# A hybrid attention and RWKV-7 layer on one core: 2 KB buffers of 2080 bytes, smaller constants, and the scores of a head pair issued ahead of the low parts of k

## The chip, the cores and the metric

The kernel runs on one core of a Trainium2 chip. The metric is the device time of one execution in microseconds (us). The kernel before took 1186.74 us, the median of 3 runs that lie between 1185.92 and 1186.84 us.

## The reference, cut to what matters

One decoder layer on 512 tokens of width 2048. The normed input goes through one input projection; its columns feed an attention with three dilations and an RWKV-7 recurrence; each branch has a gate; one output projection follows, then the residual and a final norm.

```python
h = rms_norm(x, norm_g[l])
proj = jnp.matmul(h, w_in[l]).astype(jnp.float32)
q, k, v, z_att, u_shift, z_rwkv = jnp.split(proj, splits, axis=-1)
att = dilated_mixture_attention(q, k, v, pos) * jax.nn.silu(z_att)
rwk = rwkv7_time_mix(u_shift, z_rwkv, ...)
mix = jnp.concatenate([att, rwk], axis=-1).astype(x.dtype)
x = x + jnp.matmul(mix, w_out[l])
return rms_norm(x, final_g)
```

Of the attention: 16 heads of 64 are taken as 8 pairs; q and k are rotated, the scores of a pair are masked, put through exp and divided by their sum, and the result is multiplied with v. Of the RWKV part only this matters here: `k = k * (1.0 + (a - 1.0) * k_a)`, with one constant `k_a` for each of 1024 channels.

## The kernel before, in words

Every float32 operand of a large matmul is split into a high part and a low part, and each product is three matmuls: `hh,whi`, `hl,whi` and `hh,wlo`, where `hh` and `hl` are the two parts of the normed input and `whi`, `wlo` those of a weight. The weights stream in by DMA as `raw` tiles; ScalarE (ACT) copies out `whi`, VectorE (DVE) subtracts to get `wlo`. The columns of the projection come in the order lora, k, r, v of the RWKV part, its gate z0 to z7 beside the recurrence, then q and k of the attention (`mm_qk`), then its gate (`mm_z`, z8 to z15), and then the output projection (`mo`, `mt`, `mh`).

Nothing on the chip picks the order of the work. The program is written out by a planner that runs while it is built. It keeps a model of every engine and queue (`Model`, `Engine`, `Tensor`, `Queue`, lines 42 to 134): each call to an engine moves that engine's modelled end and notes when its result will be ready. The main stream issues the large matmuls one after the other; after each, the side jobs whose time has come by the model are run a step further. A side job is a generator; `yield lat, a, b` means that it goes on when the model's clock has reached the modelled readiness of `a` and `b` plus `lat`. Which of DVE and ACT takes a copy out of PSUM, and which side job comes next, is decided by these modelled times. So a change of a modelled time by a tenth of a microsecond can move instructions anywhere behind it. On the chip each engine runs its own list in the order in which it was issued, and waits by semaphores.

The side jobs that matter here:

- `assemble` (from line 994) builds q or k of a pair: 8 DMAs on the queue of SyncE (SP) move rows of the rotated tiles `m` into `qa` or `ka`; for k, ACT then copies `kd` (high part) and DVE subtracts `kl` (low part).
- `att` (from line 1029) handles two pairs in units of 128 queries: score matmuls `s` (from `q` with `kd`, then with `kl`), a mask and maximum on DVE (`nm`), exp on ACT (`ss`, its sum `den`), a division on DVE, transposes on TensorE (`pt`), copies of these by ACT into `pa` and `pb`, and, two units behind the last one, the product `po` from `pa` and `pb`. The first unit of a pair waits by line 1043.
- `gate_g` loads a piece `gw` of a weight, splits it into `gh`, `gl` and issues four matmuls `pg`. `gate` evacuates a z into `zz` and `zt` and multiplies it with a row of y or with its attention output `yl`, which comes back from DRAM by DMA.

Most intermediates live in two rotating sets of buffers, 20 slots of 2 KB (`k2`) and 9 slots of 4 KB (`k4`). A new tile takes the slot that came free longest ago, and its first writer waits for the last reader of the slot's old content.

Of the kernel before, what the change touches and what calls it, by code (L numbers as in the profile page):

```python
# [11 lines left out]
F32 = mybir.dt.float32  # L12
F32R = mybir.dt.float32r
I32 = mybir.dt.int32
AF = mybir.ActivationFunctionType
ALU = mybir.AluOpType
# [4 lines left out]
P = 128  # L21
# [11 lines left out]
PV = {}  # L33
# [5 lines left out]
NPV = _o  # L39
# [97 lines left out]
def hymba_kernel(ctx: ExitStack, tc: tile.TileContext, xT, x, wa, wb, wo, pv, w2a2, g2, fg,  # L137
                 cst, rope, amask, bmask, out):
    nc = tc.nc
    ctx.enter_context(tc.manual_schedule())  # L140
    model = Model()
    V = Engine(model, nc.vector, 0.07, 0.00106, 0.18)
    S = Engine(model, nc.scalar, 0.06, 0.00095, 0.25)
# [6 lines left out]
    cp = ctx.enter_context(tc.tile_pool(name="cp", bufs=1))  # L150
    wp = ctx.enter_context(tc.tile_pool(name="wp", bufs=3))
    kp = ctx.enter_context(tc.tile_pool(name="kp", bufs=1))
# [5 lines left out]
    K1N, K2N, K4N, RAWN, AHEAD = 5, 20, 9, 2, 2  # L158

    def k2(shape, name, dt=F32):  # L160
        t = kp.tile([P, 528], dt, tag="k2", bufs=K2N, name=name)
        t = t[:, 0:math.prod(shape[1:])]
        return t if len(shape) == 2 else t.rearrange("p (a b) -> p a b", b=shape[2])

    def k1(shape, name, dt=F32):
        return kp.tile(shape, dt, tag="k1", bufs=K1N, name=name)
# [1 line left out]
    def k4(shape, name, dt=F32):  # L168
        return kp.tile(shape, dt, tag="k4", bufs=K4N, name=name)

    def ps(name, shape=(P, 512)):
        return pp.tile(list(shape), F32, tag="ps", name=name)

    def small(shape, name, bufs=12, dt=F32):
        return sp.tile(shape, dt, tag=f"s{shape[1]}", bufs=4 if shape[1] == 4 else bufs, name=name)

    pvt = cp.tile([P, 112], F32, name="pvt")
    nc.scalar.dma_start(pvt[:, 0:NPV], pv)

    def col(n, i):  # L180
        return pvt[:, PV[n] + i:PV[n] + i + 1]
# [5 lines left out]
    gmask = [csts[:, 320:448], csts[:, 448:576]]  # L187
    bmt = cp.tile([P, 2 * P], F32, name="bmt")
    ones = k2([P, P], "ones")
    V.memset(ones, 1.0)  # L190
    bonesr = cp.tile([P, P], F32R, name="bonesr")
    hw0 = cp.tile([P, 32], F32, name="hw0")
    omu = cp.tile([P, 27], F32, name="omu")
    V.tensor_scalar(omu, pvt[:, 0:27], -1.0, 1.0, ALU.mult, ALU.add)
    warm = small([P, 1], "warm")
    S.activation(warm, ones[:, 0:1], AF.Tanh)

    hth, htl, normed = [], [], []
    rstd = cp.tile([P, T], F32, name="rstd")
    rtok = cp.tile([P, 16], F32, name="rtok")[:, 0:4]  # L200
    xt_b, xq_b, Lb = [], [], []

    def prologue():
        acc = k2([P, T], "acc")
        xs = []

# [49 lines left out]
    def later():  # L256
        bones = k2([P, P], "bones")
        Q.dma_start(bones, cst[:, 576:704])
        Q.dma_start(bmt, bmask)
        yield 1.59, bones  # L260
        V.tensor_copy(bonesr, bones)
        V.tensor_scalar(hw0[:, 0:16], pvt[:, PV["w0"]:PV["w0"] + 16], 0.5, None, ALU.mult)
        V.tensor_scalar(hw0[:, 16:24], pvt[:, PV["k_a"]:PV["k_a"] + 8], -1.0, None, ALU.mult)
        for i in range(2):
            G.memset(xt_b[i], 0.0)
            G.tensor_copy(Lb[i][H[i], :, H[i]], ident[H[i], H[i]][:, None, :].to_broadcast([64, NCH, C]))
            yield 0.5, G
# [136 lines left out]
    def start(gen, *wait, rank=1):  # L404
        sides.append([gen, wait_for(*(wait or (0.0,))), rank])
# [161 lines left out]
    def spill_out(key, t):  # L567
        d = dp.tile([P, T], F32, name=f"sp_{key}")
        Q.dma_start(d, t)
        spill[key] = d  # L570
# [57 lines left out]
    def pre(p, r, k, v):  # L628
# [35 lines left out]
        a = k2([P, T], f"a{p}")  # L664
# [44 lines left out]
        V.tensor_scalar(rn2, rn2, 1e-24, None, ALU.max)  # L709
        V.reciprocal(rn2, rn2)  # L710
        start(subst(p, Mp, rn2), 0.06, Mp, rn2, rank=-1)
        S.activation(a, a, AF.Identity, bias=hw0[:, 16 + p:17 + p], scale=col("k_a", p))
        V.scalar_tensor_tensor(k, a, 1.0, k, ALU.add, ALU.mult)
        rk = k2([P, T], f"rk{p}")
        V.scalar_tensor_tensor(rk, r, col("r_k", p), k, ALU.mult, ALU.mult)
# [212 lines left out]
    def att_mask(t):  # L928
        return (am[0][:, 0:128], am[0][:, 128:384], am[1][:, 0:384], am[2])[t]
# [99 lines left out]
    def two(pa, t):  # L1029
        o = 256 if t == 3 else 0  # L1030
        return pa[:, o:o + 768].rearrange("p (j c) -> p j c", j=2)[:, :, t * P - o:t * P - o + P]

    def att(g):
        units = [(2 * g + pr_, t) for pr_ in range(2) for t in range(4)]
        po, ssb_, pts = {}, {}, {}
        for u in range(len(units) + 2):
            if u < len(units):
                pair, t = units[u]
                while pair not in ready or (t == 0 and u == 0 and pair >= 2 and pair - 1 not in scored):
                    yield 0.5  # L1040
                tl_ = pairs[pair]
                if t == 0:
                    yield 0.1, tl_["q"], tl_["kl", 0], tl_["kl", 1]
                n = max(256, 128 * (t + 1))
                nv = 128 * (t + 1)
                tsl = slice(t * P, (t + 1) * P)
                for h in range(2):
                    sc = ps(f"s{pair}{h}{t}")
                    TE.matmul(sc[:, 0:n], tl_["q"][:, h, tsl], tl_["k", h][:, 0:n], start=True, stop=False)
                    TE.matmul(sc[:, 0:n], tl_["q"][:, h, tsl], tl_["kl", h][:, 0:n], start=False, stop=True)  # L1050
                    ss = k2([P, T], f"ss{pair}{h}{t}")
                    nm = small([P, 1], f"nm{pair}{h}{t}")
                    V.tensor_tensor_reduce(ss[:, 0:nv], sc[:, 0:nv], att_mask(t), -0.125, 3.0e38,
                                           ALU.add, ALU.min, accum_out=nm)
                    den = small([P, 1], f"den{pair}{h}{t}")
                    S.activation(ss[:, 0:nv], ss[:, 0:nv], AF.Exp, bias=nm, scale=-1.0, accum_out=den)
                    ssb_[u, h] = (ss, den)
                if t == 3:
                    scored.add(pair)
            if u >= 2:  # L1060
                pair, t = units[u - 2]
                if t == 3:
                    po[pair] = pm.tile([P, T], F32, tag="mm", name=f"po{pair}")
                    for j in range(4):
                        for h in range(2):
                            hd = (2 * pair + h) * 64
                            pa, pb = pts[pair, h]
                            pj = (pa[:, 0:512], pa[:, 512:896], pb[:, 0:256], pb[:, 256:384])[j]
                            TE.matmul(po[pair][H[h], j * P:T], vt[j][:, hd:hd + 64], pj,
                                      start=(j == 0), stop=(j == 3))  # L1070
                if t == 3:
                    if f"s{pair}" in spill:
                        o = yl.pop(pair)
                        V.tensor_tensor(o, o, po.pop(pair), ALU.mult)
                    else:
                        o = k2([P, T], f"o{pair}")
                        S.copy(o, po.pop(pair))
                    spill_out(f"o{pair}", o)
                elif t == 2 and f"s{pair}" in spill:
                    fetch_y(pair, f"s{pair}")  # L1080
            if 1 <= u <= len(units):
                pair, t = units[u - 1]
                for h in range(2):
                    ss, den = ssb_.pop((u - 1, h))
                    if t == 0:
                        pts[pair, h] = (k4([P, 1024], f"pa{pair}{h}"), k2([P, T], f"pb{pair}{h}"))
                    pa, pb = pts[pair, h]
                    pt = ps(f"pt{pair}{h}{t}")
                    for j in range(t + 1):
                        TE.transpose(pt[:, j * P:(j + 1) * P], ss[:, j * P:(j + 1) * P], ident)  # L1090
                    if t == 0:
                        S.copy(pa[:, 0:P], pt[:, 0:P])
                    else:
                        S.copy(two(pa, t),
                               pt[:, 0:2 * P].rearrange("p (j c) -> p j c", j=2))
                    if t >= 2:
                        S.copy(pb[:, (t - 2) * P:(2 * t - 3) * P], pt[:, 2 * P:(t + 1) * P])
            yield 0.0, S
            if u < len(units):
                for h in range(2):  # L1100
                    ss, den = ssb_[u, h]
                    nv = 128 * (units[u][1] + 1)
                    V.reciprocal(den, den)
                    V.tensor_scalar(ss[:, 0:nv], ss[:, 0:nv], den, None, ALU.mult)
            yield 0.0, V
# [13 lines left out]
    def fetch_y(idx, key):  # L1119
        y = k2([P, T], f"yl{idx}")  # L1120
        Q.dma_start(y, spill[key])
        yl[idx] = y
# [53 lines left out]
            yield 1.05  # L1176

    fgt = []
    ssq = cp.tile([P, 4, 8], F32, name="ssq")
    yt = {}  # L1180

    def residual(nb):
# [247 lines left out]
```

## Time and profile before

| what | value |
|---|---|
| median of 3 runs | 1186.74 us |
| the profiled execution | 1185.99 us |
| its span, first to last instruction | 1183.9 us |
| TensorE (PE) busy | 1146.4 us, 97% of the span |
| DVE busy | 735.2 us, 62% |
| ACT busy | 568.6 us, 48% |
| GpSimd (POOL) busy | 336.4 us, 28% |
| mean granted TensorE clock | 0.993 of full |

Rows of a timeline give the start, the duration, the engine, the line in the code, the operation with its output and inputs, and in brackets the idle time ahead of it and what ended it. All engine instructions go through one helper and so share line 88 or 121 (matmuls); tiles are told apart by name. Buffer numbers are left out of the names.

### The profile page before, as it was taken

What the parts mean: (1) busy time and instruction counts of PE and PEld (TensorE: products, weight loads), DVE (VectorE), ACT (ScalarE), POOL (GpSimd) and SP (SyncE); (2) the same over time, 40 slices, a digit from 0 to 9 for tenths busy, and PEclk for the clock granted to TensorE, in tenths of its full rate; (3) what the DMA queues carried; (4) which work ended last, traced back from release to release, by engine and by line L of the source; (5) the groups of instructions that cost most, each with busy time, mean ns of one, the idle gap of its engine ahead of it and who ended that gap; (6) DMA issues with size and microseconds to landing.
All of it is one profiled execution on the core that took longest, in us unless ns stands there. A gap on an engine that the chain in (4) does not pass through costs nothing. (4 is left out here: it accounts for less than half of the span.)

```text
span 1183.9 us, 19123 instructions
## 1 busy us (share of the span) xinstructions
PE 1146.4 (97%) x6878; PEld 938.2 (79%) x6878; DVE 735.2 (62%) x1511; ACT 568.6 (48%) x1254; POOL 336.4 (28%) x586
## 2 busy tenths in 40 slices
PE   7999999999999999999999999999996999999997
PEld 5788777777787777777899977777875778888897
DVE  6667887787767957768743457665655566243252
ACT  6455665645558464564433345544443445232143
POOL 1004885647328470754630001101010000011020
PEclk9999999999999999999999999999998999999999
DMA  7334333242342525234242454433452336444343
GB/s 260 118 92 130 120 105 84 84 126 84 94 136 73 139 65 151 77 100 114 59 121 59 118 166 133 132 109 116 134 142 84 116 113 213 125 125 129 103 125 143
DMA packets 89870, 139.62 MB, mean 118 GB/s; under 512 B 37936, under 2 KB 47664, under 8 KB 89776
## 3 DMA queue, kind: packets, MB, share of 16 engines
q1 hardware_dynamic: 89344, 137.83, 39.1%
q8 instruction: 54, 0.88, 0.3%
q10 hardware_dynamic: 432, 0.58, 0.1%
q14 instruction: 40, 0.33, 0.1%
HBM read 114.44 MB, written 14.75 MB: 109 GB/s over the span
## 5 line engine op out<-in xcount | busy, mean ns | idle before, releaser
L88 POOL TENSOR_TENSOR Xtmp<-XT,Mp 128x248 f32<-128x248 f32 (+30 forms) x248 | 128.9, 520 | 143.6 <-DVE XT L88 112.8
L88 POOL TENSOR_TENSOR XT<-XT,Xtmp 128x248 f32<-128x248 f32 (+30 forms) x248 | 144.6, 583 | 21.4 <-DVE XT L88 2.5
L121 PE MATMUL mm_z<-hh,wlo 128*128 128x512 f32 x256 | 104.1, 407 | 0.0
L121 PE MATMUL mm_z<-hl,whi 128*128 128x512 f32 x256 | 103.2, 403 | 0.0
L121 PE MATMUL mm_qk<-hh,whi 128*128 128x512 f32 x256 | 102.2, 399 | 0.8 <-ACT gtok L88 0.8
L121 PE MATMUL mm_qk<-hl,whi 128*128 128x512 f32 x256 | 102.8, 401 | 0.0
L121 PE MATMUL mm_z<-hh,whi 128*128 128x512 f32 x256 | 102.7, 401 | 0.0
L88 DVE TENSOR_TENSOR wlo<-raw_o,whi 128x512 fp32r<-128x512 f32 x64 | 48.0, 790 | 87.6 <-ACT whi L88 87.6
L121 PE MATMUL mm_qk<-hh,wlo 128*128 128x512 f32 x256 | 102.1, 399 | 0.0
L88 POOL TENSOR_TENSOR y<-y,fg 128x512 f32<-128x512 f32 (+1 forms) x16 | 19.3, 1237 | 272.0 <-ACT mo L88 214.1
L88 ACT ACTIVATE whi<-raw_o 128x512 fp32r<-128x512 f32 x64 | 36.8, 623 | 96.5 <-PE mo L121 73.2
L88 POOL TENSOR_TENSOR m<-m,m 128x512 f32<-128x512 f32 x16 | 22.9, 1451 | 197.7 <-DVE m L88 92.5
L88 ACT ACTIVATE ss<-ss,nm 128x128 f32<-128x128 f32 (+3 forms) x64 | 35.5, 556 | 87.0 <-DVE nm L88 87.0
L121 PE MATMUL mo<-whi,ml 128*128 128x512 f32 x192 | 75.8, 395 | 0.0
L121 PE MATMUL mo<-whi,mh 128*128 128x512 f32 x192 | 75.8, 395 | 0.0
L121 PE MATMUL mo<-wlo,mh 128*128 128x512 f32 x192 | 75.8, 395 | 0.0
L88 DVE TENSOR_TENSOR wlo<-raw_v,whi 128x352 fp32r<-128x352 f32 (+1 forms) x80 | 50.3, 655 | 35.2 <-ACT whi L88 33.9
L88 DVE TENSOR_TENSOR wlo<-raw_z,whi 128x512 fp32r<-128x512 f32 x64 | 48.1, 771 | 33.2 <-ACT whi L88 32.9
L88 DVE TENSOR_TENSOR wlo<-raw_qk,whi 128x512 fp32r<-128x512 f32 x64 | 46.5, 745 | 32.2 <-ACT whi L88 32.1
L121 PE MATMUL mv<-whi,hh 128*128 128x352 f32 x192 | 62.7, 327 | 1.5 <-DVE m L88 1.5
L88 ACT ACTIVATE whi<-raw_v 128x352 fp32r<-128x352 f32 (+1 forms) x80 | 40.8, 542 | 46.5 <-PE mv L121 33.5
L121 PE MATMUL mv<-wlo,hh 128*128 128x352 f32 x192 | 62.2, 324 | 0.0
(303 smaller groups left out, 3043.8 us busy)
## 6 DMA issues: line engine op xcount, KB each, us to landing
raw_z<-in_wa_dram SPq DMA_DIRECT2D x32, 512.0 KB
raw_qk<-in_wa_dram SPq DMA_DIRECT2D x32, 512.0 KB
raw_o<-in_wo_dram SPq DMA_DIRECT2D x32, 512.0 KB
raw_v<-in_wb_dram SPq DMA_DIRECT2D x24, 352.0 KB
raw_r<-in_wa_dram SPq DMA_DIRECT2D x16, 512.0 KB
raw_v<-in_wa_dram SPq DMA_DIRECT2D x16, 512.0 KB
raw_k<-in_wa_dram SPq DMA_DIRECT2D x15, 512.0 KB
xk<-in_xT_dram SPq DMA_DIRECT2D x16, 256.0 KB
```

What stands on the lines that cost most here:

```text
L88: return fn(o, *args, **kw)
L121: return fn(o, lhs, rhs, **kw)
```

## The change

The `k2` slots, 2112 bytes long before (a tile of 528 floats of which a part was used), are tiles of the asked shape; the largest of them has 8 x 65 floats, so the slots become 2080 bytes. Five constants lose unused columns or get tiles of their own: `pvt` 448 to 396 bytes, `rtok` 64 to 16, `ssq` 128 to 80, and `warm` moves from one set of small tiles to the constants. The scaled constants from `w0` and `k_a`, which shared the tile `hw0`, go into two tiles: `hw0` (64 bytes) and a new `nka` of 256 bytes per partition, of which 8 columns are used. In `att` the first unit of a pair waits for `kl` of both heads alone, no longer for `q`, and with a latency of -1.5 in place of 0.1: it may be issued 1.5 us ahead of the time at which the model has `kl` ready.

```diff
     def k2(shape, name, dt=F32):
-        t = kp.tile([P, 528], dt, tag="k2", bufs=K2N, name=name)
-        t = t[:, 0:math.prod(shape[1:])]
-        return t if len(shape) == 2 else t.rearrange("p (a b) -> p a b", b=shape[2])
+        return kp.tile(shape, dt, tag="k2", bufs=K2N, name=name)
...
-    pvt = cp.tile([P, 112], F32, name="pvt")
-    nc.scalar.dma_start(pvt[:, 0:NPV], pv)
+    pvt = cp.tile([P, NPV], F32, name="pvt")
+    nc.scalar.dma_start(pvt, pv)
...
-    hw0 = cp.tile([P, 32], F32, name="hw0")
+    hw0 = cp.tile([P, 16], F32, name="hw0")
+    nka = cp.tile([P, 64], F32, name="nka")
...
-    warm = small([P, 1], "warm")
+    warm = cp.tile([P, 1], F32, name="warm")
...
-    rtok = cp.tile([P, 16], F32, name="rtok")[:, 0:4]
+    rtok = cp.tile([P, 4], F32, name="rtok")
...
-        V.tensor_scalar(hw0[:, 0:16], pvt[:, PV["w0"]:PV["w0"] + 16], 0.5, None, ALU.mult)
-        V.tensor_scalar(hw0[:, 16:24], pvt[:, PV["k_a"]:PV["k_a"] + 8], -1.0, None, ALU.mult)
+        V.tensor_scalar(hw0, pvt[:, PV["w0"]:PV["w0"] + 16], 0.5, None, ALU.mult)
+        V.tensor_scalar(nka[:, 0:8], pvt[:, PV["k_a"]:PV["k_a"] + 8], -1.0, None, ALU.mult)
...
-        S.activation(a, a, AF.Identity, bias=hw0[:, 16 + p:17 + p], scale=col("k_a", p))
+        S.activation(a, a, AF.Identity, bias=nka[:, p:p + 1], scale=col("k_a", p))
...
                 if t == 0:
-                    yield 0.1, tl_["q"], tl_["kl", 0], tl_["kl", 1]
+                    yield -1.5, tl_["kl", 0], tl_["kl", 1]
...
-    ssq = cp.tile([P, 4, 8], F32, name="ssq")
+    ssq = cp.tile([P, 4, 5], F32, name="ssq")
```

The numbers of instructions on PE, POOL and SP stay. What moves is their order, at three places below. Names carry a number of the pair, the head and the unit (`s602`: pair 6, head 0, unit 2), and at their end a running number of the tile.

The first place is the first score of pair 0, where `mm_qk10` ends. On TensorE before:

```order
L121 MATMUL mm_qk10_7255<-hh15_222,wlo101_7225 128x512
L121 MATMUL mm_qk11_7400<-hh0_106,whi102_7291 128x512
L121 MATMUL mm_qk11_7400<-hl0_107,whi102_7291 128x512
L121 MATMUL mm_qk11_7400<-hh0_106,wlo102_7292 128x512
L121 MATMUL mm_qk11_7400<-hh1_118,whi102_7291 128x512
L121 MATMUL s000_7413<-kd_000_7374,q_00_7329 128x256
L121 MATMUL s000_7413<-kl_000_7375,q_00_7329 128x256
```

On TensorE now, the same scores:

```order
L121 MATMUL mm_qk10_7256<-hh14_217,wlo101_7226 128x512
L121 MATMUL s000_7388<-kd_000_7375,q_00_7330 128x256
L121 MATMUL s000_7388<-kl_000_7376,q_00_7330 128x256
L121 MATMUL s010_7396<-kd_001_7379,q_00_7330 128x256
L121 MATMUL s010_7396<-kl_001_7380,q_00_7330 128x256
L121 MATMUL mm_qk10_7256<-hh15_223,whi101_7225 128x512
L121 MATMUL mm_qk10_7256<-hl15_224,whi101_7225 128x512
L121 MATMUL mm_qk10_7256<-hh15_223,wlo101_7226 128x512
```

The scores moved up by seven of the large matmuls. On DVE behind the same scores, before (`g32s` belongs to the gates' weights, `ISA` is the mask and maximum):

```order
L88 TENSOR_TENSOR kl_001_7379<-ka_001_7284,kd_001_7378 128x512
L88 TENSOR_TENSOR m0_10_7403<-mm_qk10_7255,L0_233 128x512
L88 TENSOR_TENSOR m3_10_7405<-mm_qk10_7255,L0_233 128x512
L88 TENSOR_TENSOR g32s_7408<-dup32_7337,g32s_7408 32x512 x2
L88 ISA ss000_7416,nm000_7417<-s000_7413,L1_236 128x128
```

And now:

```order
L88 TENSOR_TENSOR kl_001_7380<-ka_001_7283,kd_001_7379 128x512
L88 ISA ss000_7391,nm000_7392<-s000_7388,L1_237 128x128
L88 ISA nm000_7392 128x1
L88 ISA ss010_7399,nm010_7400<-s010_7396,L1_237 128x128
L88 ISA nm010_7400 128x1
L88 TENSOR_TENSOR g32s_7416<-dup32_7338,g32s_7416 32x512 x2
```

The mask and maximum of unit 0 moved ahead of `g32s`.

The second place is SP's queue where q and k of pair 7 (`qa_31x`, `ka_31x`) are put together. Before, behind the first six of the eight `qa` transfers:

```order
L133 DMA qa_311_9262<-m0_30_8633 32x512
L133 DMA qa_311_9262<-m2_30_8747 32x512
L133 DMA ka_310_9267<-m0_31_8882 32x512
L133 DMA ka_310_9267<-m2_31_9056 32x512
L133 DMA ka_310_9267<-m0_31_8882 32x512
L133 DMA ka_310_9267<-m2_31_9056 32x512
L133 DMA ka_311_9272<-m0_31_8882 32x512
L133 DMA ka_311_9272<-m2_31_9056 32x512
L133 DMA ka_311_9272<-m0_31_8882 32x512
L133 DMA ka_311_9272<-m2_31_9056 32x512
L133 DMA gw2_9296<-in_g2_dram 128x128
```

Now, from the same transfer on:

```order
L133 DMA qa_311_9221<-m0_30_8624 32x512
L133 DMA qa_311_9221<-m2_30_8786 32x512
L133 DMA raw129_z10_9238<-in_wa_dram 128x1024
L133 DMA raw130_z11_9295<-in_wa_dram 128x1024
L133 DMA gw2_9323<-in_g2_dram 128x128
L133 DMA gw2_9323<-in_g2_dram 32x128 x4
L133 DMA yl10_9331<-sp_y2_3824 128x512
L133 DMA ka_310_9333<-m0_31_8925 32x512
L133 DMA ka_310_9333<-m2_31_9099 32x512
```

The eight `ka` transfers no longer stand right behind the eight `qa` transfers; two weight loads and the inputs of the third gate stand between them.

The third place is TensorE in `mm_z10`, around the matmuls `pg2` of the third gate and the product `po5` of pair 5. Before, where the eight matmuls of `po5` end five rows ahead of the first row here:

```order
L121 MATMUL s602_9518<-kd_300_9203,q_30_9008 128x384
L121 MATMUL s602_9518<-kl_300_9204,q_30_9008 128x384
L121 MATMUL s612_9526<-kd_301_9207,q_30_9008 128x384
L121 MATMUL s612_9526<-kl_301_9208,q_30_9008 128x384
L121 MATMUL pt601_9534<-csts_82,ss601_9390 128x128 x2
L121 MATMUL pt611_9538<-csts_82,ss611_9398 128x128 x2
L121 MATMUL mm_z10_9442<-hl10_193,whi129_9362 128x512
L121 MATMUL mm_z10_9442<-hh10_192,wlo129_9363 128x512
L121 MATMUL mm_z10_9442<-hh11_198,whi129_9362 128x512
L121 MATMUL mm_z10_9442<-hl11_199,whi129_9362 128x512
L121 MATMUL pg2_9550<-g128h_5527,gh2_9302 128x512
L121 MATMUL pg2_9550<-g128l_5528,gh2_9302 128x512
```

Now, where `s602` follows 18 large matmuls behind the end of `po5`:

```order
L121 MATMUL mm_z10_9405<-hh10_193,wlo129_9360 128x512
L121 MATMUL pg2_9505<-g128h_5528,gh2_9329 128x512
L121 MATMUL pg2_9505<-g128l_5529,gh2_9329 128x512
L121 MATMUL pg2_9505<-g128h_5528,gl2_9330 128x512
L121 MATMUL pg2_9505<-g32s_7416,gl2_9330 128x512
L121 MATMUL mm_z10_9405<-hh11_199,whi129_9359 128x512
L121 MATMUL po5_9512<-pa50_9048,vt0_6096 64x512
L121 MATMUL po5_9512<-pa51_9053,vt0_6096 64x512
L121 MATMUL po5_9512<-pa50_9048,vt1_6097 64x384
L121 MATMUL po5_9512<-pa51_9053,vt1_6097 64x384
```

`pg2` moved from behind `s602` and `pt601` to a place ahead of `po5`.

## Rows read from the trace of the kernel before

**Rows 1.** The page's busy time of each engine.

```profile
PE 1146.4 (97%) x6878; PEld 938.2 (79%) x6878; DVE 735.2 (62%) x1511; ACT 568.6 (48%) x1254; POOL 336.4 (28%) x586
```

**Rows 2.** Stretches: length, busy PE, PEld, DVE, ACT, POOL; granted clock, DMA share, GB/s.

```profile
5.00:10.00 5.00, 4.68 (x11) 3.17 (x12) 2.42 (x5) 2.39 (x5) 0.00 (x0) 1.00 0.98 352
...
150.00:225.00 75.00, 71.07 (x584) 56.06 (x583) 59.60 (x111) 46.96 (x99) 48.70 (x90) 1.00 0.37 100
850.00:950.00 100.00, 89.64 (x420) 70.08 (x419) 56.32 (x149) 43.80 (x126) 2.97 (x2) 0.93 0.40 118
```

**Rows 3.** TensorE's waits: line, releaser, total us, times, longest.

```profile
PE zpb L121 <- DVE xnb L88: 2.7, 2, 1.7
...
PE s L121 <- DVE kl L88: 1.0, 2, 0.7
```

**Rows 4.** Timeline of TensorE, 892 to 898 us.

```profile
892.13 1.94 PE L121 MATMUL pt<-csts,ss 128*128 128x128 f32 x8 [3.73 <-DVE den L88]
...
896.00 0.63 PE L121 MATMUL mm_z<-hh,whi 128*128 128x512 f32 x1
896.43 0.63 PE L121 MATMUL mm_z<-hl,whi 128*128 128x512 f32 x1
...
897.26 0.39 PE L121 MATMUL mm_z<-hh,whi 128*128 128x512 f32 x1
```

**Rows 5.** Timeline of TensorE, 855 to 857 us.

```profile
855.74 0.28 PE L121 MATMUL s<-kl,q 128*128 128x256 f32 x1
855.86 1.03 PE L121 MATMUL pt<-csts,ss 128*128 128x128 f32 x8
856.65 0.47 PE L121 MATMUL mm_qk<-hl,whi 128*128 128x512 f32 x1
```

**Rows 6.** Timeline of DVE, from 887 us.

```profile
887.81 0.69 DVE L88 TENSOR_TENSOR zz<-mm_z,rstd 128x512 f32<-128x512 f32 x1 [4.67 <-DMA ka<-m]
```

**Rows 7.** Timeline of SP's queue, 876 to 888 us.

```profile
877.02 4.94 SPq L133 DMA_DIRECT2D qa<-m  x8
882.07 4.96 SPq L133 DMA_DIRECT2D ka<-m  x8
```

**Rows 8.** Timeline of TensorE, 910 to 922 us.

```profile
910.62 0.87 PE L121 MATMUL pt<-csts,ss 128*128 128x128 f32 x4 [0.72 <-DVE den L88]
...
917.40 0.76 PE L121 MATMUL pg<-g128h,gh 128*128 128x512 f32 x1 [4.98 <-DVE nm L88]
...
921.26 0.39 PE L121 MATMUL mm_z<-hl,whi 128*128 128x512 f32 x1
```

**Rows 9.** Timeline of ACT and of DVE, 904 to 918 us.

```profile
907.29 0.27 ACT L88 COPY pa<-pt 128x128 f32<-128x128 f32 x1 [9.61 <-PE po L121]
...
908.12 0.69 DVE L88 TENSOR_TENSOR wlo<-raw_z,whi 128x512 fp32r<-128x512 f32 x1 [11.43 <-ACT whi L88]
```

**Rows 10.** Timeline of all engines, 699 to 709 us.

```profile
700.48 0.39 PE L121 MATMUL s<-kl,q 128*128 128x256 f32 x1 [0.36 <-DVE kl L88]
...
708.53 0.70 PE L121 MATMUL pt<-csts,ss 128*128 128x128 f32 x2 [0.92 <-DVE den L88]
```

**Rows 11.** Timeline of all engines, 820 to 831 us.

```profile
824.56 0.69 DVE L88 TENSOR_TENSOR yl<-yl,po 128x512 f32<-128x512 f32 x1 [7.91 <-DMA yl<-sp_s]
...
829.74 0.39 PE L121 MATMUL s<-kl,q 128*128 128x256 f32 x1 [0.66 <-DVE kl L88]
```

**Rows 12.** DVE groups by line and form: count, busy us, mean ns, idle before.

```profile
L88 DVE TENSOR_TENSOR zz<-mm_z,rstd 128x512 f32<-128x512 f32 x16 | 11.0, 687 | 8.5 <-DMA ka<-m 4.7 <-PE mm_z L121 3.7
L88 DVE TENSOR_TENSOR u_k<-mm_k,rstd 128x512 f32<-128x512 f32 x8 | 5.5, 686 | 1.2 <-PE mm_k L121 1.2
```

**Rows 13.** Timeline of TensorE, from 215 us.

```profile
215.49 0.69 PE L121 MATMUL zpb<-xnb,mo 32*32 32x32 f32 x32 [1.65 <-DVE xnb L88]
...
216.46 0.39 PE L121 MATMUL mm_z<-hh,whi 128*128 128x512 f32 x1
216.68 0.40 PE L121 MATMUL mm_z<-hl,whi 128*128 128x512 f32 x1
```

## The prediction

> **What bounds the kernel now.** I read the busy times of the engines first. TensorE is busy 97% of the span, the next engine, DVE, 62% [rows 1]. So the time is TensorE's work plus TensorE's idle time, 1183.9 - 1146.4 = 37.5 us, and a change that leaves the matmuls alone can only move these 37.5 us and the speed at which the matmuls run. Then I read the stretches, to see where the idle time lies. Some of it is the start (the first weights) and the end (the last norm), which no edit here is meant for. The largest piece by far is 850 to 950 us, the end of the attention with the gates z8 to z10: 100 - 89.64 = 10.4 us idle, and the granted clock is 0.93 there, which is some 14 us at the lower of the two levels, 1.2 instead of 2.4 GHz [rows 2]. The worst stretch of the recurrence, 150 to 225, has 3.9 us [rows 2].
>
> The timeline shows what the piece at 850 to 950 is made of. Two stalls make nearly all of it.
>
> Stall A. The transposes `pt` at 892.13 waited 3.73 us for the division on DVE [rows 4]. DVE was not slow: its evacuation `zz` had waited 4.67 us for the DMAs `ka` to finish reading [rows 6], because `zz` got a buffer slot whose old content, a rotated `m` tile, those DMAs still had to read, and all DVE work behind it stood. They read late since SP's queue holds the eight `qa` transfers and then the eight `ka` transfers back to back, 4.94 and 4.96 us of issuing [rows 7]. After the stall the clock is at the lower level: large matmuls start 0.43 us apart at 896.00, against 0.23 in the rows at full clock [rows 4, 13]. From 892.13 to 897.26 TensorE ran eight transposes, five large matmuls, four score matmuls of 256 columns and two more transposes. At full clock the eight transposes take 0.79 us and a score matmul 0.12 us [rows 5], so that work is 0.79 + 5 x 0.23 + 4 x 0.12 + 0.2 = 2.6 us; it took 5.13. Stall A costs 3.7 + 2.5 = 6.2 us.
>
> Stall B. ACT's copy `pa` of pair 6 waited 9.61 us for `po5`, the last reader of its slot; ACT's weight copies stood behind it, so DVE's `wlo` waited 11.43 us [rows 9]. When both went on, DVE had a backlog, and `pg2` on TensorE, which stands behind the new scores, waited 4.98 us for a score buffer that DVE had to read first [rows 8]. From 917.40 to 921.26 nine large matmuls took 3.86 us, 9 x 0.23 = 2.1 at full clock, so 1.8 more. Stall B costs 5.0 + 1.8 = 6.8 us.
>
> **The change part by part.** No part adds or removes a matmul, and the split of `hw0` adds no instruction. What the edits do is move: the two small DVE writes to `hw0` were modelled as dependent (the second 0.12 us after the first), now they are not, and a shift of 0.12 us in the model deals out the whole program anew behind the first microseconds; the new `yield` moves the attention. I cost the new order at the places where the old one stalled.
>
> Stall A. SP's queue now has two weight loads, the third gate's inputs and `yl10` between the `qa` and the `ka` transfers of pair 7, as the second place of the order shows. With the slots dealt out anew, the `zz` of z8 gets a slot that a score tile `ss` used, free long before, and its `zt` one whose reader is DVE itself. So DVE has nothing to wait for there. I take the whole 6.2 us as gained. The gain is not below 0, since the stall is there now, and not over 6.2.
>
> Stall B. `pg2` now stands ahead of `po5` and of the new scores (third place), and its weight split stands ahead of the evacuation of z9 on DVE. It no longer needs what the backlog delays: gain 6.8 us. What is late next is the same copy `pa`, which still waits for `po5`, by my count of columns some 5.6 us in place of 10; behind it the divisions for `pt` of unit 1, now 18 large matmuls (4.2 us) behind `po5`, end about when TensorE gets there. Today's `pt` behind the same copy waited 0.72 us [rows 8]. I take 0.7 as its price, with 0 below and 5.0 (what `pg2` waited) above.
>
> The early scores. At pair 0 they move up by seven large matmuls, 7 x 0.23 = 1.6 us, the difference of the two latencies. But `kl` is there when the `ka` transfers let it be, and today's scores already wait 0.36 us for it [rows 10]. TensorE works in order, so the seven matmuls now stand behind the wait: 0.36 + 1.6 = 2.0 us, a loss of 1.6. At pair 4 the wait for `kl` is 0.66 us [rows 11], 1.0 in all with pair 0 [rows 3]; DVE stood there 7.9 us for `yl`, whose load was queued behind 16 transfers, and the load now comes earlier in SP's queue. One moves against the other; I take nothing, between a gain of 0.8 and a loss of 1.6. Pairs 2 and 6 do not wait today [rows 3], and in the new order the `ka` transfers of pair 2 stand ahead of those of q: nothing, at most 1.6 each. Dropping `q` from the wait costs nothing: its parts are made before those of k.
>
> What the early scores give: their mask on DVE now stands ahead of `g32s` at pair 0 (first place), and the transposes that waited 0.92 us [rows 10] should not. Gain 0.9.
>
> The addresses. Slots of 2080 bytes begin at odd multiples of 32 every second time, those of 2112 never did. The nearest row is an evacuation that writes 4 bytes off the slot's start: `u_k` takes 686 ns, `zz` at the start of a slot 687 [rows 12]. So DVE gets 0, and any loss of DVE or ACT is hidden at 62% and less. The large matmuls stream `hh`, `hl` and `whi`, none of which is such a slot.
>
> The weight tiles `raw` now begin 128 bytes past a multiple of 256, and the transfers run full only at the start, with a DMA share of 0.98 in 5 to 10 us [rows 2]. The Trainium skill, "DMA: Bandwidth & Descriptors", section "How a descriptor splits into AXI transactions", says that a transaction must begin at a multiple of 256 bytes, so a row that does not costs one more. By it, a 2 KB row would take nine for eight, and the start would be longer by an estimated 0.3 us. No row here has both starts side by side; the sum leaves it out.
>
> The recurrence. Its order is shuffled by one to a few matmuls throughout. The tight hand-overs are about as many as before. I take 0, with 4 us to either side, what its worst stretch holds now [rows 2].
>
> **Sum.** Gains 6.2 + 6.8 + 0.9 = 13.9; losses 1.6 + 0.7 = 2.3; net 11.6 us. 1185.99 of the profiled execution less 11.6 is 1174.4; the median of the runs lies 0.75 above that execution, so 1175.1 us.
>
> **The rivals.** 0.2% is 2.4 us, about what a measurement of this kernel can tell from no change.
>
> First rival, give-back. The old order was one deal of the planner, the new one is another, and A and B were its accidents. New ones of the same kind (a slot whose reader is late, a DVE queue behind it) can stand where I saw none. For it: the planner's model is blind to what made A, the real landing of 16 transfers. Against: the recurrence's longest wait is 1.7 us [rows 3], so a common accident costs 1 to 2 us, and six or more are needed. Half given back, 1180 to 1184; all, 1184.4 to 1189, about 1186.
>
> Second rival, slower. The early scores are issued before their data at pairs 0, 2, 4 and 6, and TensorE stands at each. If the transfers, ACT and DVE deliver `kl` later against the model than at pair 0, each pair waits not 1.6 but some 4 us more, and a wait as long as A's 3.73 was followed by the lower clock, another 2 us (one of 1.65 us was not [rows 13]). Four pairs at 6 us are 24, less the 11.6 + 1.6 that the sum has: 1186.7 + 11, 1198. It decides against the gain from 3.3 us a pair on. Against it: only two pairs of eight wait at all now, 1.0 us together [rows 3].
>
> Third rival, the addresses matter after all. Score, transpose and `po` matmuls read slots of which half now lie off. There are 128 score matmuls of 0.12 to 0.23 us, some 20 us, and I reckon as much again for the others. If half of these 40 us ran 10% longer, that would be 2 us: 1177. It also ends within the forecast's own range.
>
> A fourth: the edit does not do what it says, since TensorE cannot run a score before `kl` is there. That is so at pair 0 in my sum, and changes nothing else; the gain comes from the new order either way.
>
> **How the numbers follow.** The forecast's own case, 1168 to 1180, third rival within: 0.58. Half given back: 0.18. All given back, no difference: 0.11. Slower, by the second rival or by more new stalls than went: 0.13. So faster 0.76, same 0.11, slower 0.13. The low end is the forecast less the recurrence's 4, less 0.8 at pair 4, 0.7 at `pt`, 1.6 at pair 0: 1168, and 1 for what I can't see: 1167. The high end reaches through most of no difference, to 1188; some 0.04 lies below and 0.13 above.
>
> **What would show it.** In the trace after: no wait of `zz` for `ka`; the stretch that holds z8 to z10 with idle time near 2 us in place of 10.4, and a granted clock at 1.00; `pg` without a wait near 5 us; `s` waiting about 2 us for `kl` at pair 0 and near none at pairs 2 and 6; no `pt` wait of 0.9 at pair 0; idle time of 0 to 620 us within 4 us of today's. I am wrong if a new wait of over 3 us with its low clock appears anywhere, above all at the scores of an even pair or at `pt` and `po` of pair 6.

## The result, and the profile after

The changed kernel takes 1155.24 us (1153.59 to 1156.83, 4 runs) against 1186.33 us of the kernel before in the same session: a ratio of 0.9739, 95% interval 0.9723 to 0.9756. It is 31 us faster. The forecast was 1175.1 us, with a range of 1167 to 1188: the sign was right and the size was not.

The busy times of the engines, from the page of the changed kernel:

```profile
span 1153.0 us, 19134 instructions
PE 1128.8 (98%) x6878; PEld 936.0 (81%) x6878; DVE 736.4 (64%) x1524; ACT 561.6 (49%) x1241; POOL 339.2 (29%) x586
```

This line splits the gain at once. TensorE's idle time went from 37.5 us [rows 1] to 1153.0 - 1128.8 = 24.2 us, 13.3 less, and its busy time, for the same 6878 matmuls, went down by 17.6 us. The forecast spoke of the first. Of the second it had only what the lower clock behind two stalls cost, 4.3 us.

The stretches of the changed kernel (length, busy PE, PEld, DVE, ACT, POOL, granted clock, DMA share, GB/s):

```profile
150.00:225.00 75.00, 72.90 (x600) 58.90 (x599) 56.95 (x110) 49.62 (x106) 49.30 (x86) 1.00 0.32 92
850.00:950.00 100.00, 99.72 (x487) 80.90 (x485) 63.98 (x161) 47.11 (x130) 2.54 (x2) 1.00 0.46 135
```

Against [rows 2], 850 to 950 lost its 10.4 us of idle time (0.3 are left) and runs at full clock, and 150 to 225 went from 3.9 to 2.1. Waits of TensorE, line and releaser with total us, times and longest; first three of the kernel before:

```profile
PE pt L121 <- DVE den L88: 5.4, 3, 3.7
PE pg L121 <- DVE nm L88: 5.0, 1, 5.0
...
PE pt L121 <- DVE yl L88: 0.9, 2, 0.7
```

Then those of the changed kernel:

```profile
PE mm_lora L121 <- ACT whi L88: 5.7, 2, 5.3
PE Y L121 <- DVE A L88: 2.0, 3, 1.2
PE Y L121 <- ACT A L88: 2.0, 5, 0.7
PE s L121 <- ACT kd L88: 0.9, 1, 0.9
PE zpb L121 <- DVE xnb L88: 0.9, 1, 0.9
...
PE pt L121 <- DVE den L88: 0.7, 2, 0.5
...
PE s L121 <- DVE kl L88: 0.4, 1, 0.4
```

The 5.0 us of `pg` and the 3.7 us of `pt` are gone; the longest wait behind the start is 1.2 us. The places of the forecast, in the timelines of TensorE, of DVE and of ACT:

```profile
691.22 0.38 PE L121 MATMUL s<-kd,q 128*128 128x256 f32 x1 [0.89 <-ACT kd L88]
692.00 0.39 PE L121 MATMUL s<-kl,q 128*128 128x256 f32 x1 [0.40 <-DVE kl L88]
...
887.76 0.39 PE L121 MATMUL pg<-g128h,gh 128*128 128x512 f32 x1
...
896.67 0.81 PE L121 MATMUL pt<-csts,ss 128*128 128x128 f32 x4 [0.28 <-DVE den L88]
...
869.34 0.68 DVE L88 TENSOR_TENSOR zz<-mm_z,rstd 128x512 f32<-128x512 f32 x1
...
890.80 0.27 ACT L88 COPY pa<-pt 128x128 f32<-128x128 f32 x1 [4.69 <-PE po L121]
```

The `zz` of z8 no longer waits for `ka` [rows 6], `pg2` does not wait [rows 8], and the copy `pa` still waits for `po5`, 4.7 us in place of 9.6 [rows 9], at the price of 0.28 us at `pt`.

What is not in the forecast shows in the output projection, where neither kernel has anything to wait for. The tile's own view lists 192 matmuls of each form, their duration in ns (least, median, most) and their first and last start; of the kernel before, then of the changed one:

```profile
L121 PE MATMUL mo<-whi,mh x192: 390/393/404, 996.1 to 1129.3; 128*128 128x512 f32 x192
```

```profile
L121 PE MATMUL mo<-whi,mh x192: 389/389/389, 967.9 to 1097.8; 128*128 128x512 f32 x192
```

The three forms take turns, so from the first of these starts to the last there are 191 x 3 = 573 intervals. Their mean is (1129.3 - 996.1) / 573 = 232.5 ns before and (1097.8 - 967.9) / 573 = 226.7 ns after. Before, durations scatter; after, every one is the same. This is the unit below: "the interval" is the mean distance from one start to the next among matmuls of 512 columns.

### The profile page after: what moved, and what is told of

It reads as the page before. It is cut to its first block, busy times and chain, and to the rows that moved or that the text cites. A ratio compares the mean times of both kernels' runs of the same rounds, so it can differ in the third digit from the quotient of the medians.

```text
span 1153.0 us, 19134 instructions
## 1 busy us (share of the span) xinstructions
PE 1128.8 (98%) x6878; PEld 936.0 (81%) x6878; DVE 736.4 (64%) x1524; ACT 561.6 (49%) x1241; POOL 339.2 (29%) x586
## 5 line engine op out<-in xcount | busy, mean ns | idle before, releaser
L88 POOL TENSOR_TENSOR Xtmp<-XT,Mp 128x248 f32<-128x248 f32 (+30 forms) x248 | 136.6, 551 | 168.3 <-DVE XT L88 151.0
L88 POOL TENSOR_TENSOR XT<-XT,Xtmp 128x248 f32<-128x248 f32 (+30 forms) x248 | 139.8, 564 | 21.4 <-DVE XT L88 2.5
L88 DVE TENSOR_TENSOR wlo<-raw_qk,whi 128x512 fp32r<-128x512 f32 x64 | 50.2, 812 | 35.2 <-ACT whi L88 35.0
L121 PE MATMUL mv<-whi,hl 128*128 128x352 f32 x192 | 62.8, 327 | 0.0
```

Of the source, the lines that this page charges most:

```text
L88: return fn(o, *args, **kw)
L121: return fn(o, lhs, rhs, **kw)
```

## The experiments

Three theories for the shorter interval: the new order (ORDER), the place of the weight tiles (WEIGHTS), the size of the slots (SLOTS). The addresses of the tiles in the two programs say what moved. The constants are 128 bytes longer in all, so `raw`, `whi` and `wlo`, which lie behind them, begin at a multiple of 256 bytes in the kernel before and 128 bytes past one in the changed one. `hh` and `hl` begin 128 past one in both, and so do `mh` and `ml`, the two parts of the mixed branches that `mo` reads: they use the same slots. "The distance" below is that of the two operand tiles of a matmul, modulo 256 bytes: 128 before, 0 after.

**Slots alone.** The edit is the change's own `k2` helper in the kernel before.

```diff
-        t = kp.tile([P, 528], dt, tag="k2", bufs=K2N, name=name)
...
+        return kp.tile(shape, dt, tag="k2", bufs=K2N, name=name)
```

> The kernel before with slots of 2080 bytes alone, no instruction moved; the weight tiles stay at a multiple of 256 bytes, only what lies behind the slots moves. Theory ORDER (the whole gain, the shorter interval of the large matmuls included, comes from the new order): within 0.2% of 1186, mean interval of the large matmuls 232 ns. Theory WEIGHTS (the interval hangs on where the tiles from the third score constant on lie, the weight tiles above all): also within 0.2% of 1186, 232 ns. Theory SLOTS (it hangs on the slot size or on what lies behind the slots): 13 to 17 us faster, about 1171, interval 227 ns.

Measured: 1187.35 us, ratio 1.0003 (0.9992 to 1.0014), interval 232 ns in `mo`. No order moved and no time moved. SLOTS falls, and the forecast's zero for the slots' odd starts holds.

**Slots, and the weight tiles moved.** One more edit:

```diff
-    ssq = cp.tile([P, 4, 8], F32, name="ssq")
+    ssq = cp.tile([P, 4, 16], F32, name="ssq")
```

> As the run before it, and one constant of 128 bytes made 256 bytes, so that the weight tiles and all behind them lie 128 bytes further, as in the changed kernel; the order is that of the kernel before. ORDER: within 0.2% of 1186, 232 ns. WEIGHTS: 13 to 17 us faster, about 1171, interval 227 ns, stalls A and B still there. SLOTS: as the run before it.

Measured: 1175.9 us, ratio 0.9901 (0.9883 to 0.9919). The order is that of the kernel before, row for row. Its busy times and two of its waits, from its page and its waits:

```profile
span 1172.5 us, 19123 instructions
PE 1131.2 (96%) x6878; PEld 935.9 (80%) x6878; DVE 734.1 (63%) x1511; ACT 568.2 (48%) x1254; POOL 337.9 (29%) x586
```

```profile
PE pt L121 <- DVE den L88: 6.2, 4, 3.9
...
PE pg L121 <- DVE nm L88: 5.0, 1, 5.0
PE zpb L121 <- DVE xnb L88: 3.9, 2, 1.9
```

Both stalls are still there, and TensorE is busy 1146.4 - 1131.2 = 15.2 us less. Its idle time is 3.8 us more (41.3 against 37.5): with faster matmuls DVE ends last more often. The wait of `pt` for `den` is 6.2 us against 5.4 and that of `zpb` 3.9 against 2.7 [rows 3]. So 128 bytes are worth 11.4 us here, under the 13 to 17 expected, mostly by what came back as idle time. ORDER falls as the cause of the interval.

**The reverse, in the changed kernel.**

```diff
-    ssq = cp.tile([P, 4, 5], F32, name="ssq")
+    ssq = cp.tile([P, 4, 13], F32, name="ssq")
```

> The changed kernel with the same constant 128 bytes longer, so that the weight tiles lie at a multiple of 256 bytes as in the kernel before; no instruction moved. ORDER: unchanged, 1155, 227 ns. WEIGHTS: 13 to 17 us slower than the changed kernel, about 1170, 232 ns, stalls A and B still gone. SLOTS: 1155.

Measured: 1167.13 us, ratio to the kernel before 0.9823 (0.9809 to 0.9838). 12 us of the gain went (13 to 17 were expected), and `mo` is back at 232.3 ns. The profiled spans add up: 1183.9 of before, -11.4 for the place alone, -18.6 for the order alone (1165.3 here), which makes 1153.9, and the changed kernel's is 1153.0.

**The old wait in the changed kernel.**

```diff
-                    yield -1.5, tl_["kl", 0], tl_["kl", 1]
+                    yield 0.1, tl_["q"], tl_["kl", 0], tl_["kl", 1]
```

> The changed kernel with the latency and the tiles of the old wait ahead of a pair's scores; all addresses as in the changed kernel, and the order of everything up to the attention. If the early scores made stalls A and B go: 8 to 13 us slower than the changed kernel, 1163 to 1168, interval 227 ns. If the re-dealt order did it, by the split of the constant: within 3 us of 1155. ORDER adds: the interval could go back to 232 ns; WEIGHTS: it stays at 227 ns.

Measured: 1172.69 us, ratio 0.9869 (0.9851 to 0.9888), so 16 to 17 us slower than the changed kernel, where 8 to 13 were expected; the interval of `mo` stays at 226.7 ns, as WEIGHTS said. Its span is 17.3 us longer, 11.2 of it idle time and 6.1 a longer busy time of TensorE (1134.9 us, with a granted clock of 0.93 in 850 to 950). Its waits of TensorE:

```profile
PE pt L121 <- DVE den L88: 6.2, 4, 3.9
PE pg L121 <- DVE nm L88: 5.0, 1, 5.0
```

Stalls A and B are back, with the constant still split. It is the new `yield` that removed them, not the new deal that came with the split. Of its two halves it is the latency: the planner writes the kernel before in the same order whether `q` stands in that line or not.

**Place or distance.** The kernel with slots of 2080 bytes, everything moved up by 128 bytes; and, in the second run, the weight tiles by 128 more (`ssq` again as above).

```diff
     kp = ctx.enter_context(tc.tile_pool(name="kp", bufs=1))
+    hp.tile([P, 32], F32, name="pad")
```

> The order of the kernel before, slots of 2080 bytes, everything moved up by 128 bytes: hh and hl now at a multiple of 256 bytes, the weight tiles 128 past one. Theory PLACE (only the weight tiles' own place counts): as in the run with the weights alone moved, about 1176, interval 227 ns. Theory DISTANCE (what counts is the distance of the weight tiles from hh and hl, modulo 256; it is 128 here as in the kernel before): about 1187, 232 ns.

> As the run before it, and the weight tiles 128 bytes further: both at a multiple of 256 bytes. PLACE: about 1187, 232 ns, as with the weights there before. DISTANCE (0 here, as in the changed kernel): about 1176, 227 ns.

Measured: 1186.85 us, ratio 0.9994 (0.9983 to 1.0005), and 1177.71 us, ratio 0.9918 (0.9889 to 0.9947). The tile's view of `mo` in the first and in the second:

```profile
L121 PE MATMUL mo<-whi,mh x192: 390/393/405, 998.0 to 1131.1; 128*128 128x512 f32 x192
```

```profile
L121 PE MATMUL mo<-whi,mh x192: 389/389/389, 991.9 to 1121.8; 128*128 128x512 f32 x192
```

133.1 / 573 = 232.3 ns and 129.9 / 573 = 226.7 ns. With the weight tiles 128 past a multiple of 256, the place that is good in the changed kernel, but `hh` and `hl` moved along, the gain is gone; with both at a multiple of 256 it is back. PLACE falls, DISTANCE stands: what counts is where the two operands of a large matmul lie to each other.

**Other distances.** `ssq` 32 and 64 bytes longer in the kernel with slots of 2080 bytes.

```diff
-    ssq = cp.tile([P, 4, 8], F32, name="ssq")
+    ssq = cp.tile([P, 4, 10], F32, name="ssq")
```

> The order of the kernel before, slots of 2080 bytes, the weight tiles moved by 32 bytes, hh and hl where they were. If only a distance of 0 against 128 counts, an interval between 227 and 232 ns, and 1176 to 1187; if any move off 128 does it, 227 ns and 1176; if only a distance of 0 is good, 232 ns and 1187.

> The same with the weight tiles moved by 64 bytes. Halfway between the two places known: 229 to 230 ns and 1181 if the interval goes evenly with the distance; 227 or 232 ns if there are two states alone; anything under 226 ns would show a place better than that of the changed kernel.

Measured: 1189.23 us, ratio 1.0014 (1.0003 to 1.0026), and 1182.29 us, ratio 0.9953 (0.9933 to 0.9972). `mo` with the tiles 32 and 64 bytes further:

```profile
L121 PE MATMUL mo<-whi,mh x192: 392/397/401, 1000.5 to 1134.7; 128*128 128x512 f32 x192
```

```profile
L121 PE MATMUL mo<-whi,mh x192: 393/396/398, 992.7 to 1126.4; 128*128 128x512 f32 x192
```

234.2 and 233.3 ns. In `mm_qk` the same means, taken over neighbouring starts of the timeline, are 232.6 (kernel before), 233.4, 229.4 and 228.0 (moved by 0, 32, 64, 128). Moved by 32 bytes both are a little worse than unmoved; by 64, `mm_qk` is between the best and the unmoved, `mo` is not. So it is neither two states nor an even slope; of the four distances tried 0 is the best, in every group of matmuls of 512 columns. That 64 bytes give 229.4 ns in one and 233.3 in the other may come from the sides: `mm_qk` streams the input part and `mo` the weight part, so the same move has the other sign there. No run tests that.

**The early scores alone, in the kernel before.** Only line 1043 is changed.

```diff
-                    yield 0.1, tl_["q"], tl_["kl", 0], tl_["kl", 1]
+                    yield -1.5, tl_["kl", 0], tl_["kl", 1]
```

> The kernel before with the new latency alone, every address as before. If the early scores alone make stalls A and B go, here as in the changed kernel: the 16 to 17 us that taking them out of the changed kernel cost, 1170 to 1171, interval 232 ns. If they need the re-dealt order of the split constant beside them: 1175 to 1187, one of the two stalls still there.

Measured: 1171.56 us, ratio 0.9872 (0.9855 to 0.9888). Two stretches of it:

```profile
75.00:225.00 150.00, 146.15 (x997) 116.20 (x996) 118.30 (x212) 89.85 (x180) 88.35 (x157) 1.00 0.38 108
...
850.00:950.00 100.00, 99.76 (x486) 79.12 (x485) 61.97 (x160) 45.31 (x128) 2.55 (x2) 1.00 0.43 127
```

The expected 1170 to 1171 us is met within the interval. The attention is clean without any other part of the change; the recurrence is as in the kernel before (75 to 225 us has 3.85 us idle). The run with the whole order at the old place (1165.3 profiled) is 3.7 below this one (1169.0): that is what the deal of the split constant gives, and it has 1.75 us idle in 75 to 225. Without the early scores, at distance 0, the same deal gives 1172.5 - 1170.3 = 2.2 us of span.

**Earlier still.** The changed kernel with -3.0 in place of -1.5 in the same line.

> The changed kernel with a latency of -3.0 in place of -1.5. If what counts is that the scores wait in TensorE's order for kl: pairs whose kl comes late wait up to 1.5 us longer each, 1156 to 1161. If what counts is only which order the planner deals: anything within 1150 to 1170, with stalls at other places; interval 227 ns either way.

Measured: 1166.64 us, ratio to the kernel before 0.9831 (0.9816 to 0.9845): 11 us slower than the changed kernel, and outside of what the first theory gave. Its waits of TensorE and the stretch they lie in:

```profile
PE s L121 <- DVE kl L88: 6.7, 4, 3.3
...
PE s L121 <- ACT kd L88: 1.8, 2, 1.3
```

```profile
700.00:850.00 150.00, 143.24 (x697) 114.53 (x696) 92.16 (x236) 68.60 (x190) 13.79 (x10) 0.98 0.42 120
```

The scores now wait 8.5 us in all against 1.3, over four waits for `kl`, the longest 3.3. The span is 11.1 us longer, 7.4 of it idle time and 3.7 busy time (1132.5). The first theory has the mechanism and half the size: it left out the lower clock. Both long waits were followed by it, with large matmuls 0.43 us apart in place of 0.23:

```profile
760.95 0.39 PE L121 MATMUL s<-kl,q 128*128 128x256 f32 x1 [2.59 <-DVE kl L88]
...
763.07 0.63 PE L121 MATMUL mm_qk<-hh,wlo 128*128 128x512 f32 x1
763.49 0.63 PE L121 MATMUL mm_qk<-hh,whi 128*128 128x512 f32 x1
...
825.73 0.39 PE L121 MATMUL s<-kl,q 128*128 128x256 f32 x1 [3.33 <-DVE kl L88]
...
828.21 0.63 PE L121 MATMUL mm_qk<-hh,whi 128*128 128x512 f32 x1
828.64 0.63 PE L121 MATMUL mm_qk<-hl,whi 128*128 128x512 f32 x1
```

Behind each wait nine intervals take 3.64 us (from 762.24 and from 827.02) in place of 9 x 0.227 = 2.0, so 1.6 us are lost twice, most of the 3.7.

**Which tile.** The kernel with slots of 2080 bytes, its two `raw` buffers 64 bytes wider each, which moves `whi`, `wlo` and what lies behind them by 128.

```diff
-            raw = self.raw.get(i) if part else wp.tile([P, 1024], F32, tag="raw", bufs=RAWN, name=f"raw{i}_{name}")
+            raw = self.raw.get(i) if part else wp.tile([P, 1040], F32, tag="raw", bufs=RAWN, name=f"raw{i}_{name}")
```

> The order of the kernel before, slots of 2080 bytes, the two raw buffers 64 bytes wider each, so that only whi, wlo and what lies behind them move by 128 bytes; gates' weights, masks and the first raw buffer stay. If the operands of the large matmuls themselves count (whi and wlo against hh and hl): 227 ns and 1176. If raw or a tile ahead of it counts, by DMA, ACT or DVE: 232 ns and 1187.

Measured: 1178.06 us, ratio 0.9925 (0.9905 to 0.9944), `mo` at 226.7 ns. The first `raw` buffer, the masks and the gates' weights lie where they lay, and the second `raw` buffer moved by 64 bytes only; the gain is there, 8.8 us in this run. So it does not hang on where the transfers into `raw` land.

**256 bytes further.** The changed kernel with `ssq` as [P, 4, 21].

> The changed kernel with everything from the third score constant on 256 bytes further. If the distance counts modulo 256: 1155 to 1156, 227 ns. If it counts modulo 512 or more: another interval, down to below 226 ns (faster) or up to 234.

Measured: 1154.35 us, ratio 0.9725 (0.9705 to 0.9744), `mo` at 226.7 ns. This cannot be told from the changed kernel's 0.9739, so a step of 256 bytes changes nothing here. A smaller power of two is ruled out as the period, since distances of 0 and 128 differ.

## Why the prediction was right in sign and wrong in size

**The step that failed** is the addresses. It said that the large matmuls "stream `hh`, `hl` and `whi`, none of which is such a slot", looked at the slots alone, and costed the addresses at 0. It had the fact in hand one sentence later, that `raw` now begins 128 bytes past a multiple of 256, and weighed it only for the DMAs. The runs give that term 11.4 us in the span at the old order and 12.3 at the new one; the two other runs that reach distance 0 are 8.8 and 9.9 us faster than the kernel before. Some 3260 matmuls of 512 columns (768 each of `mm_z` and `mm_qk`, 576 of `mo`, 384 each of `mm_k`, `mm_r`, `mm_v`) start 4 to 6 ns closer together, which comes to some 15 us of busy time (15.2 measured), and 3.8 us of it come back as idle time. The row that it leaned on was of DVE [rows 12]; it had no row of TensorE with another distance of its operands, and should have kept a bound for one. With 3260 matmuls, 1% of an interval is 7.6 us. The third rival saw addresses matter, but on the wrong tiles (scores and transposes). Without this term the time would have come to lie at the low end of the range: the run with the whole order and the weight tiles put back took 1167.13 us. And none of the signs that the forecast named could have shown the miss, since all of them are waits, idle time and the granted clock, none the busy time of TensorE; they came about as said.

**The order**, forecast at 11.6 us net, gave 18.6 in the span of the run with the weight tiles put back. Of that, 14.9 came with the early scores and 3.7 with the deal of the split constant.

- Stalls A and B, 13.0 us: both went, as said, by the means said (`zz` free at once, `pg2` ahead of `po5`). It had left open which of the two edits did it, and booked the early scores themselves at 0.9 of gain against 1.6 of loss. They went with the latency alone, and stayed when only the split was there.
- The lower clock: it costed 4.3 us. With the early scores alone TensorE's busy time fell by 1146.4 - 1141.2 = 5.2 us.
- The wait of `pt` at pair 0, 0.9: gone as said; one of 0.46 us stands at a later unit in the changed kernel.
- The wait at pair 0 for `kl`: forecast 2.0 us in all, measured 0.89 + 0.40 = 1.3 in the changed kernel, a loss of 0.9 and not 1.6; ACT's `kd` ended part of it.
- The wait at `pt` behind the copy `pa`: forecast 0.7, measured 0.28, with the copy's own wait 4.7 us where 5.6 was counted.
- Pair 4: costed at nothing; its wait went, and so did two waits of `pt` for `yl`, 0.9 us together in the kernel before, which were not in the sum.
- The recurrence: 0 with 4 to either side. The idle time of 0 to 620 us went from 16.2 to 13.2 in the changed kernel, and to 12.0 in the run with the weight tiles put back, so it gave 3 to 4, at the bound. That is the largest part by which the order was underrated. The stretch before, then changed:

```profile
0.00:620.00 620.00, 603.80 (x4009) 486.08 (x4010) 451.71 (x872) 345.53 (x698) 298.78 (x557) 1.00 0.38 111
```

```profile
0.00:620.00 620.00, 606.80 (x4116) 495.59 (x4117) 456.16 (x890) 341.81 (x692) 301.54 (x557) 1.00 0.38 112
```

**The rivals.** Give-back did not come: no new wait above 1.2 us. The second rival, scores that wait for `kl`, is real but did not decide at -1.5; at -3.0 it costs 8.5 us of waits and 11 us of time, with the lower clock that the rival had foretold. Its remark that the wait of 1.65 us was not followed by the lower clock is true of that execution alone: with only the slots changed, the same wait was followed by it (granted 0.98 in 150 to 225 us), with large matmuls 0.43 us apart:

```profile
215.95 0.69 PE L121 MATMUL zpb<-xnb,mo 32*32 32x32 f32 x32 [1.58 <-DVE xnb L88]
...
217.82 0.63 PE L121 MATMUL mm_z<-hh,whi 128*128 128x512 f32 x1
218.25 0.63 PE L121 MATMUL mm_z<-hl,whi 128*128 128x512 f32 x1
```

The third rival is answered above. The fourth is right as far as it goes: at pair 0 the scores wait for `kd` and `kl`, and the gain comes from the order that the latency makes. The sentence on the transactions of unaligned rows, from the Trainium skill's "DMA: Bandwidth & Descriptors", section "How a descriptor splits into AXI transactions", would have the start an estimated 0.3 us longer. No run here shows it: the first wait of `mm_lora` is 5.3 us in both kernels, and over all the runs it lies between 5.1 and 5.9 us, so 0.3 could not be told.

## What to carry to other kernels

When an edit changes the size of a tile, list what lies behind it and look at every pair of tiles that an engine reads together, not only at the tile itself: here 128 bytes in a constant's size were worth 1% of the kernel. A busy engine is not one at its peak: where the busy time changes with the same instructions, compare the distance between starts in a stretch without waits before any wait is explained. And a side job that is issued a little ahead of its data can pay for the wait it makes by what it frees behind it, up to a point that has to be measured (-1.5 against -3.0). Before a mean is called unchanged, ask what it is a mean of: `mv` below has the same mean in both kernels to 0.1 ns, because it is the same mixture.

## What the runs showed of the hardware that was not expected

- Matmuls of 128 x 512 float32r, back to back at the full granted clock, start (in `mo`) 226.7 ns apart when the tiles of the two operands lie at the same place modulo 256 bytes, and 232.4 ns apart when they differ by 128; 32 bytes more make it 234.2.
- Shorter matmuls go the other way, by less. `mh`, 256 columns, goes from distance 128 to 0 with the change, and its median duration rises from 281 to 283 ns; by neighbouring starts its interval rises from 120.0 to 121.4 ns. Before, then changed:

```profile
L121 PE MATMUL mh<-wlo,mh x64: 274/281/285, 1130.1 to 1153.2; 128*128 128x256 f32 x64
```

```profile
L121 PE MATMUL mh<-wlo,mh x64: 277/283/283, 1098.6 to 1122.0; 128*128 128x256 f32 x64
```

- `mt`, also 256 columns, reads its weights from the `k4` slots behind the 20 `k2` slots. Slots shorter by 32 bytes move these by 640 bytes, 2.5 x 256, so `mt` has distance 0 in the run with the slots alone; with the 128 bytes of the constants on top it has 128 again in the changed kernel. Its interval is 118.7 ns before and after the change, and 120.0 with the slots alone. Before, then with the slots alone:

```profile
L121 PE MATMUL mt<-whi,mh x64: 279/281/285, 1153.5 to 1175.9; 128*128 128x256 f32 x64
```

```profile
L121 PE MATMUL mt<-whi,mh x64: 280/283/283, 1153.3 to 1176.0; 128*128 128x256 f32 x64
```

- `mv` has 352 columns, rows of 1408 bytes, 5.5 x 256, two in a weight tile. So half of its matmuls have distance 0 and half 128 in both kernels, and the mean over all does not move. Taken apart, and without the intervals of 180 ns and more, in which something else stands, the halves are 158.4 (128) and 160.1 ns (0) in the kernel before, 158.5 (128) and 160.2 (0) in the changed one, where they have changed places.
- With a distance of 0 every interval of `mo` is 226 or 227 ns; with 128 they run from 228 to 241 in a repeating row. At the same distance of 128, the run with the early scores alone had 233.3 ns in `mo` in place of 232.4; the rows do not explain it. Why the distance matters, why its sign turns with the number of columns, which of the two reads gives way, and whether it is a matmul's own weights or those loaded for the next one that count, is not shown by any run here.
